# Three attention stages whose VectorE and ScalarE queues take the order of the source

## The chip, the cores and the metric

The program runs on one core of a Trainium2 chip, in one launch. The metric is the device time of one execution in microseconds. Before the change the median of three runs was 4061.31 us (4060.87 to 4061.83). All times below come from these runs or from one profiled execution of the kernel before.

## The reference, cut to what matters

Two blocks of two layers each work on 512 tokens and 256 context tokens of width 1024, batch 1, float32. The first layer of the first block is a recurrent mixer (RWKV); it is not touched. Behind it stand three attentions:

```python
# layer 2 of block 1 (MLA): 16 heads, 512 queries, 768 keys (tokens and context)
s = q @ k.T / sqrt(96);  p = softmax(s);  o = p @ v;  d_x = (o * silu(gate)) @ w_out

# layer 1 of block 2 (AB): 8 heads with a window of 128, 256 context keys and a sink column in the softmax,
# and 8 heads over all 768 keys; tokens (512) and context (256) are both queries; 2 kv heads in each half
q = rope(rms_norm(q) * g);  k = rope(rms_norm(k) * g)
p = softmax(concat([s_local, s_ctx, sink]));  o = p @ v;  o_lat = concat(oa, ob) @ w_out

# layer 2 of block 2 (C): 8 heads, each with two score matrices over the 768 keys
a = softmax(s[0]) - lam * softmax(s[1]);  o = rms_norm(a @ v) * (1 - lam_init);  o_lat = o @ w_out
```

Behind AB and behind C stands a mixture of 32 experts, of which each token takes two.

## The kernel before, in words

The kernel is written in a tile language. Each statement is an instruction for one engine; a planner then sets the order in which each engine's queue takes its instructions, by its own costs, and adds the semaphores. A block `with tc.manual_schedule(engines=...)` tells the planner to leave the named engines in the order of the source for what stands in the block. Before the change the three attentions name `PEO`, which is TensorE (PE) alone: PE runs in the order of the source, while VectorE (DVE), ScalarE (ACT), GpSimd (POOL) and SyncE (SP, which issues most DMAs) run in the planner's order. Other blocks of the kernel already name more engines (the products behind the attentions that lead to an expert layer name PE, DVE and ACT, L1707).

**What each attention does.** A unit of work is a *query tile of 128 rows of one head* ("item"). For it PE writes scores into a PSUM tile `S` (two of them), DVE takes the row maximum (L1261, in C L2760) and scales it (L1263, L2761), ACT makes the exponentials and their sum (L1268, L2763), DVE takes the reciprocal of the sum (L1272, L2766) and scales the probabilities (L1277, L2417, L2768). In the source these stand together, one behind the other. PE then transposes the probabilities of an *earlier* item (two items earlier in MLA and AB, one in C), DVE and ACT take turns to copy the transposes out of PSUM (L1296 on ACT, L1298 on DVE, L2778), and when a head is full PE multiplies with the values.

**What fills PE between.** `Fill` (L2069) holds generators that make the projections of the *next* pair of heads (MLA, `mla_project`), the next unit of four heads (AB, `AbUnit.all`; four units) or the next head (C, `CHead.all`; eight heads). `fill()` is called once or several times per item and issues a few matmuls each time. Where a projection tile is complete, its consumers are issued at that very place of the source: ACT copies, and in AB and C the norm of queries and keys with their rotation, `qk_split` (L2666, "the norm" below): a square on ACT (L2674), a sum on DVE (L2676), twelve short DVE instructions that follow each other (L2677, L164 to L168), a scaling (L2679), then products on DVE (L2689) and POOL (L2690, L2691) whose sum DVE takes (L2692), and a split into a high and a low part (L2693, L2694). AB has three norms in each of its first three units, C three in each of its first seven heads. Their transposes follow later (`turns`, L2286; `turns_c` and `turns_x`, L2633 on), with casts into `Q` and `K` by DVE and ACT in turn.

**The weights of C.** `CHead.all` calls `CIn.later` (L2571), which splits the weights of the head after next into a high and a low part, in four pieces:

```python
for i in range(4):
    if i:
        self.load(h, i)              # a DMA into one of two buffers (WB = 2)
    with self.g.tc.issue_after(after.ins):
        self.split(h, i)             # ACT: cast to the high part (L2546); POOL: the low part (L2547)
```

Pieces 2 and 3 can be loaded only when POOL has let go of the buffers of pieces 0 and 1. In the source the four casts stand one behind the other, ahead of the exponentials of the second query tile. The weights of AB are split by POOL (L2211, L2212), behind the last projection tile of a unit.

Of the kernel before, what the change touches and what calls it, by code (L numbers as in the profile page):

```python
# [1367 lines left out]
def fresh(g, i):  # L1368

    g.R[i] = g.place(i, [P, D], F32)  # L1370
    return g.R[i]
# [259 lines left out]
def take_in(g, into, tiles):  # L1631

    with g.tc.tile_pool(name="psIn", bufs=2, space=PSUM) as ps, g.tc.manual_schedule(engines=PEO):
        into.pre(tiles[0])
# [69 lines left out]
def last_products(g, nxt, OT, wo, tiles):  # L1704
    moe = isinstance(nxt, MoeIn)
    with g.tc.tile_pool(name="psPo", bufs=3, space=PSUM) as ps, \
            g.tc.manual_schedule(engines=PEO | ({mybir.EngineType.DVE, mybir.EngineType.Activation} if moe else set())):  # L1707
        if moe:
            nxt.finish(ps, OT, wo)
        else:  # L1710
            out_last(g, ps, OT, wo, tiles, lambda i, *ps: nxt.turn(i, *ps) if ps else nxt.pre(i))
# [141 lines left out]
def mla_layer(g, into, nxt):  # L1853
    nc, tc, I = g.nc, g.tc, g.I
    s = into
    kp = s.outs.enter_context(tc.tile_pool(name="mlK", bufs=1, reuse_waits="tile"))
    s.OT = kp.tile([P, 8, NX], F32, name="OTl")
    s.wl = kp.tile([P, D], F32, name="wl")
    with tc.tile_pool(name="mlP", bufs=2, reuse_waits="tile") as s.pp, tc.tile_pool(name="mlT", bufs=3, reuse_waits="tile") as s.pt, \
            tc.tile_pool(name="ringP", bufs=2, reuse_waits="tile") as s.ring, \  # L1860
            tc.tile_pool(name="psS2", bufs=2, space=PSUM, reuse_waits="tile") as s.pss, tc.tile_pool(name="psT2", bufs=2, space=PSUM, reuse_waits="tile") as s.pst, \
            tc.tile_pool(name="psU2", bufs=2, space=PSUM, reuse_waits="tile") as s.psu:
        s.P, s.att, s.got = {}, 0, 0
        fill = Fill()
        fill.add(mla_project(g, s), 1)
        with tc.manual_schedule(engines=PEO):
            for pr in range(8):
                fill.until(lambda: pr in s.P)
                s.att = pr
                if pr == 7:  # L1870
                    mla_out(g, s, fill, nxt)
                mla_attend(g, s, pr, fill)
            fill.drain()
    into.close()
    nxt.early()
    nxt.open()
    with tc.tile_pool(name="psPo", bufs=2, space=PSUM) as ps, tc.manual_schedule(engines=PEO):
        for i in range(2):
            nxt.pre(i)
        nxt.turn(0, ps)  # L1880
        out_last(g, ps, s.OT, lambda i: s.wl, g.R[2:], lambda i, *ps: None if ps else nxt.pre(i + 2))
        for i in range(1, 6):
            nxt.turn(i, ps)
    nxt.full()
    s.outs.close()
# [177 lines left out]


PEO = {mybir.EngineType.PE}
HIM = -4096


# [264 lines left out]
def ab_layer(g, into, nxt):  # L2333
    nc, tc, I = g.nc, g.tc, g.I
    MC = g.M2[0]
    s = into
    with tc.tile_pool(name="abO", bufs=1, reuse_waits="tile") as kp, tc.tile_pool(name="abQ", bufs=1, reuse_waits="tile") as qp:
        s.OT = OT = kp.tile([P, 8, NT], F32, name="OT")
        s.got = 0
        with tc.tile_pool(name="abP", bufs=2, reuse_waits="tile") as s.pp, tc.tile_pool(name="psS2", bufs=2, space=PSUM, reuse_waits="tile") as s.pss, \  # L2340
                tc.manual_schedule(engines=PEO):
            s.place(1)
            s.split(1, True)
            s.room = True
            cur = s.first.place(qp)
            for i in range(3):
                cur.turns(i)
            for u in range(4):
                fill = Fill()
                s.room = False  # L2350
                if u == 1:
                    s.tables(1)
                if u < 3:
                    ahead = AbUnit(s, u + 1).place(qp)
                    fill.add(ahead.all(fill), ABN)
                else:
                    ahead = None
                    s.back()
                    ring = [s.ring.tile([P, 8 * 384], F32, name="wao", tag=n) for n in ("raw", "high", "low")]
                    wo = [ring[k // 3][:, k % 3 * D:k % 3 * D + D] for k in range(8)]  # L2360
                    for k in range(8):
                        for c in range(2):
                            nc.sync.dma_start(wo[k][:, c * 512:c * 512 + 512], I["ab_out"][c][:, k])
                    hf = s.pool.tile([P, 8 * NT], F32, name="hf", tag="hT")
                    G_ = [hf[:, i * D:i * D + D] for i in range(2)]
                    for i in range(2):
                        row_bcast(g, s.psu, MC, 16, 3 - i, G_[i], "pu")

                    both = [qp.tile([P, 2 * NT], F32, name="wl", tag=n, bufs=b) for n, b in (("Qab", 3), ("Kab", 2))]
                    wl = [w[:, 0:D] for w in both]  # L2370
                    if isinstance(nxt, MoeIn):
                        nxt.prepare([w[:, D:] for w in both], s.psu, "pu", fill.later)
                    for v in range(2):
                        nc.gpsimd.tensor_tensor(out=wl[v], in0=wo[7], in1=G_[v], op=ALU.mult)
                    fill.add(out_heads(g, s.psu, OT, wo, g.R, [G_[0]] * 2 + [G_[1]] * 4, [hf[:, k * 512:k * 512 + 512] for k in range(4, 8)],
                                       lambda: min(s.got, 7) if s.got >= 6 else 0, 7), 73000)
                ab_attend(g, s, cur, ahead, fill)
                fill.drain()
                if u < 3:
                    cur = ahead  # L2380
        into.close()
        nxt.early()
        nxt.open()
        last_products(g, nxt, OT, lambda i: wl[int(i > 1)], g.R)
        nxt.full()
# [312 lines left out]
def c_layer(g, into, nxt):  # L2698
    nc, tc, I = g.nc, g.tc, g.I
    MC = g.M2[1]  # L2700
    s = into
    with tc.tile_pool(name="cK", bufs=1, reuse_waits="tile") as kp, tc.tile_pool(name="cP", bufs=2, reuse_waits="tile") as s.pp:
        s.OT = OT = kp.tile([P, 8, NX], F32, name="OT")
        with tc.tile_pool(name="psS2", bufs=2, space=PSUM, reuse_waits="tile") as s.pss, \
                tc.manual_schedule(engines=PEO):
            cur = s.first.place(s.pp)
            for h in range(8):
                fill = Fill()
                if h < 7:
                    ahead = CHead(s, h + 1).place(s.pp)  # L2710
                    fill.add(ahead.all(fill), 21000)
                else:
                    s.back()
                    last, Gx = (fresh(g, i) for i in range(2))
                    w = [s.tile("wco", n, F32).rearrange("p a k f -> p a (k f)") for n in ("low1", "low0", "high1", "high0")]
                    wo = [w[k // 3][:, k % 3] for k in range(7)] + [last]
                    for k in range(8):
                        for c in range(2):
                            nc.sync.dma_start(wo[k][:, c * 512:c * 512 + 512], I["c_out"][c][:, k])
                    row_bcast(g, s.psu, MC, 16, 2, Gx, "pu")  # L2720
                    nc.gpsimd.tensor_tensor(out=last, in0=last, in1=Gx, op=ALU.mult)
                    if isinstance(nxt, MoeIn):
                        nxt.prepare([s.pp.tile([P, 2 * NT], F32, name="rw", tag="Kc")], s.psu, "pu", fill.later)
                    fill.add(out_heads(g, s.psu, OT, wo, g.R[2:], [Gx] * 4, [w[3][:, 1 + k // 2, k % 2 * 512:k % 2 * 512 + 512] for k in range(4)],
                                       lambda: 0 if s.left else 7, 7), 48000)
                if h == 0:
                    cur.turns_c()
                    for _ in range(16):
                        fill.one()
                    cur.turns_x()  # L2730
                c_attend(g, s, h, cur, fill)
                fill.drain()
                if h < 7:
                    cur = ahead
            c_finish(g, s)
        into.close()
        nxt.early()
        nxt.open()
        last_products(g, nxt, OT, lambda i: last, g.R[2:])
        nxt.full()  # L2740
# [668 lines left out]
```

## Time and profile before

| what | value |
|---|---|
| time, median of 3 runs | 4061.31 us |
| profiled execution: its own time | 4052.4 us |
| profiled execution: span from first to last instruction | 4050.6 us |
| MLA attention, 1476 to 1826 us of the span | 350 us, PE busy 333.1, DVE 211.4 |
| AB attention, 1902 to 2281 us | 379 us, PE busy 345.0, DVE 270.9 |
| C attention, 3015 to 3409 us | 394 us, PE busy 352.3, DVE 256.9 |

The span is read along one clock that starts with the first instruction. An engine's busy time is the time in which at least one of its instructions ran; what is left is time in which it waited. The granted clock of TensorE (PEclk) is the mean share of its full speed in a stretch. In the timeline, the bracket behind an instruction is the idle time of its engine ahead of it and what ended it.

### The profile page before, as it was taken

How to read it: one execution, taken by the hardware profiler on the slowest of the kernel's cores; microseconds unless marked ns; L12 is line 12 of the kernel's file. 1: busy time of each engine (PE TensorE's matmuls, PEld its weight loads, DVE VectorE, ACT ScalarE, POOL GpSimd, SP SyncE). 2: the span in 40 equal slices, each digit the busy share in tenths (PEclk: the TensorE clock that was granted, in tenths of full speed). 3: DMA queues.
4: the chain of work that ended last, by engine and by line, in shares of the span. 5: the costliest groups of instructions: out<-in, count | busy, mean ns of one | idle time of the engine just before them, and what ended most of it. 6: DMA issues, size and time to landing. Idle time of an engine off the chain costs nothing. (4 is left out here: it accounts for less than half of the span.)

```text
span 4050.6 us, 83636 instructions
## 1 busy us (share of the span) xinstructions
PE 3554.0 (88%) x34840; PEld 2257.8 (56%) x34840; DVE 2120.0 (52%) x5084; ACT 1285.9 (32%) x3117; POOL 756.0 (19%) x745
## 2 busy tenths in 40 slices
PE   7699899989878889997899789999868888999998
PEld 4677777777764467656775432232268884322322
DVE  6434544455455666648885643333377774433333
ACT  3243344334322354424443211111145542111110
POOL 1100000000001111121211233333232221322221
PEclk9799998999978899998999899999979998999999
DMA  6865565666564110112011489999731123999995
GB/s 210 232 187 187 180 201 179 207 197 194 187 200 136 69 58 31 42 65 72 23 46 36 161 322 371 394 380 377 264 99 43 48 88 133 351 384 375 374 372 213
DMA packets 282440, 778.76 MB, mean 192 GB/s; under 512 B 62348, under 2 KB 183244, under 8 KB 255820
## 3 DMA queue, kind: packets, MB, share of 16 engines
q1 hardware_dynamic: 258460, 710.63, 49.0%
q0 software_dynamic: 19552, 56.67, 5.0%
q8 instruction: 275, 4.51, 0.5%
q10 hardware_dynamic: 4048, 6.10, 0.4%
q14 instruction: 105, 0.86, 0.1%
HBM read 715.57 MB, written 71.86 MB: 194 GB/s over the span
## 5 line engine op out<-in xcount | busy, mean ns | idle before, releaser
L3189 PE MATMUL H<-wex,xT 128*32 128x512 f32 x3072 | 561.3, 609 | 56.1 <-DMA wex<-in_w 50.9
L3190 PE MATMUL H<-wex,xT 128*32 128x512 f32 x1024 | 539.1, 610 | 11.4 <-DMA wex<-in_w 11.4
L3192 PE MATMUL H<-wex,xT 128*32 128x512 f32 x2048 | 537.2, 602 | 0.0
L3148 PE MATMUL Y<-wex,uT 128*32 128x512 f32 x2048 | 507.9, 596 | 2.9 <-issue 1.7
L3189 PEld LDWEIGHTS H<-wex,xT 128*32 128x32 f32 x3072 | 127.4, 112 | 329.8 <-issue 260.4
L3161 DVE TENSOR_TENSOR yo<-R,Y 64x512 f32<-64x512 f32 x128 | 87.4, 684 | 388.5 <-PE Y L3148 201.7
L3154 PE MATMUL Yc<-wex,uT 128*32 128x512 f32 x1024 | 288.0, 614 | 0.0
L3090 POOL DMA_INDIRECT xg<-hbuf,rq x192 | 184.5, 961 | 544.6 <-DVE xT L3098 420.8
L411 PE MATMUL pd<-dw,dl 128*128 128x128 f32 x1536 | 249.7, 307 | 33.9 <-DMA dl<-Ld 24.3
L3192 PEld LDWEIGHTS H<-wex,xT 128*32 128x32 f32 x2048 | 121.2, 112 | 243.1 <-issue 236.5
L411 PEld LDWEIGHTS pd<-dw,dl 128*128 128x128 f32 x1536 | 210.0, 210 | 54.7 <-DMA dl<-Ld 21.4
L411 PE MATMUL pd<-dl,dw 128*128 128x128 f32 x1344 | 215.9, 297 | 5.4 <-issue 1.7
L1268 ACT ACTIVATE prob<-S,smx 128x768 f32<-128x768 f32 (+3 forms) x160 | 125.7, 786 | 237.0 <-DVE smx L1263 208.7
L1206 DVE COPY RT<-ZU 32x128 f32<-32x128 f32 x192 | 54.4, 283 | 260.9 <-PE ZU L411 233.6
L411 PEld LDWEIGHTS pd<-dl,dw 128*128 128x128 f32 x1344 | 175.8, 198 | 27.1 <-issue 10.2
L2611 PE MATMUL pu<-wc,hT 128*128 128x384 f32 (+1 forms) x768 | 181.4, 324 | 0.0
L3117 ACT COPY uT<-puT 128x384 f32<-128x384 f32 x64 | 30.7, 479 | 469.4 <-PE puT L3115 469.4
L3166 DVE TENSOR_TENSOR yo<-R,Yc 32x512 f32<-32x512 f32 x128 | 87.6, 684 | 166.1 <-PE Yc L3154 165.1
L1261 DVE TENSOR_REDUCE smx<-S 128x1 f32<-128x768 f32 (+3 forms) x160 | 128.8, 805 | 69.1 <-PE S L1999 38.3
L3098 DVE STREAM_TRANSPOSE xT<-xg 128x768 f32<-128x768 f32 (+1 forms) x68 | 102.9, 1514 | 114.2 <-PE H L3192 92.5
L3106 ACT ACTIVATE th<-H 128x512 f32<-128x512 f32 x64 | 38.2, 597 | 374.8 <-PE H L3190 367.4
L1231 ACT ACTIVATE RT<-SY,PC 64x64 f32<-64x64 f32 x368 | 93.8, 303 | 152.8 <-PE SY L411 148.1
(623 smaller groups left out, 7950.8 us busy)
## 6 DMA issues: line engine op xcount, KB each, us to landing
wex<-in_w SPq DMA_DIRECT2D x186, 2048.0 KB, 13.9
dl<-Ld SPq DMA_DIRECT2D x180, 512.0 KB, 4.1
wmod<-in_mod_w SPq DMA_DIRECT2D x128, 512.0 KB, 4.8
dw<-in_rw_in SPq DMA_DIRECT2D x30, 512.0 KB, 7.4
wex<-in_w POOLq DMA_DIRECT2D x6, 2048.0 KB, 11.3
wcr<-in_c_in SPq DMA_DIRECT2D x28, 384.0 KB, 4.1
Ld<-lerp SPq DMA_DIRECT2D x18, 512.0 KB, 6.0
lerp<-in_mod_w SPq DMA_DIRECT2D x8, 1024.0 KB, 13.1
```

Of the source, the lines that this page charges most:

```text
L411: return g.nc.tensor.matmul(out, **kw)
L1231: ev = nc.scalar.activation(nrt[h, d, ni if d == 0 else 3 - ni, e, :], Sp[h, d, :], AF.Copy, scale=PC[h, d, cc[d]:cc[d] + 1])
L1261: nc.vector.tensor_reduce(m[:, 0:1], S[:, :n], mybir.AxisListType.X, ALU.max)
L1268: nc.scalar.activation(p[:, :n], S[:, :n], AF.Exp, scale=scale, bias=m[:, 1:2], accum_out=m[:, 2:3])
L2611: nc.tensor.matmul(o, lhsT=x, rhs=w[:, a:3, kb, :], start=kb == i == 0, stop=kb == 7 and i == 2)
L3090: own.gather = nc.gpsimd.indirect_dma_start(out=xg[:, a], out_offset=None, in_=quarters, in_offset=bass.IndirectOffsetOnAxis(ap=own.rq[:, ...
L3098: own.turned = nc.vector.transpose(xT[:, a:a + n].rearrange("p a k t -> p (a k) t"), xg[:, a:a + n].rearrange("p a (i k) -> p a k i", k=8))
L3148: mm(self.Y[h][q(self.lb + a)], lhsT=self.uT[:, fb, q(a)], rhs=self.w2[:, fb, 512 * h:512 * h + 512], start=fb == 0, stop=fb == 3)
L3154: mm(self.Yc[q(self.hb + h)], lhsT=self.uT[:, fb, q(2)], rhs=self.w2[:, fb, 512 * h:512 * h + 512], start=fb == 0, stop=fb == 3)
L3189: mm(H1[q(to)], lhsT=xT[:, a, kb, :], rhs=w[0][:, kb, :], **f)
L3190: mm(H1[q(lb + 1)], lhsT=xT[:, 2, kb, :], rhs=w[1][:, kb, :], **f)
L3192: mm(H3[q(hb + a)], lhsT=xT[:, a, kb, :], rhs=w[1][:, kb, :], **f)
```

## The change

In the three places where an attention's block is opened, the set of engines that keep the order of the source grows from PE to PE, DVE and ACT. POOL and SP stay with the planner. No instruction is added or taken away by the text of the change; what stands ahead of the blocks and behind them is planned as before.

```diff
@@ mla_layer
-        with tc.manual_schedule(engines=PEO):
+        with tc.manual_schedule(engines=PDA):
             for pr in range(8):
                 fill.until(lambda: pr in s.P)
@@
 PEO = {mybir.EngineType.PE}
+PDA = PEO | {mybir.EngineType.DVE, mybir.EngineType.Activation}
 HIM = -4096
@@ ab_layer
-                tc.manual_schedule(engines=PEO):
+                tc.manual_schedule(engines=PDA):
             s.place(1)
             s.split(1, True)
@@ c_layer
-                tc.manual_schedule(engines=PEO):
+                tc.manual_schedule(engines=PDA):
             cur = s.first.place(s.pp)
             for h in range(8):
```

## Rows read from the trace of the kernel before

**Rows 1.** Busy time by stretch: three stages, one MLA pair, one AB unit.
```profile
core 0: us, PE busy (x) PEld busy (x) DVE busy (x) ACT busy (x) POOL busy (x), PEclk, DMA share, GB/s
...
1476.00:1826.00 350.00, 333.09 (x1762) 230.01 (x1761) 211.35 (x477) 145.29 (x279) 53.35 (x44) 0.98 0.14 45
1902.00:2281.00 379.00, 345.00 (x2045) 257.94 (x2044) 270.86 (x772) 144.84 (x370) 75.84 (x83) 0.94 0.09 29
3015.00:3409.00 394.00, 352.34 (x2107) 300.46 (x2106) 256.89 (x769) 175.36 (x447) 91.70 (x100) 0.95 0.19 53
1513.00:1553.00 40.00, 37.09 (x213) 26.79 (x213) 25.21 (x54) 17.96 (x35) 6.15 (x4) 1.00 0.09 30
1902.00:1987.00 85.00, 73.38 (x484) 62.28 (x483) 69.13 (x214) 34.68 (x94) 20.87 (x30) 0.89 0.05 14
```

**Rows 2.** DVE timeline, AB (start, us, instruction, idle before): reciprocals behind 513, 768, 256 columns.
```profile
1905.89 0.16 DVE L1272 RECIPROCAL smx<-smx 128x1 f32<-128x1 f32 x1 [0.91 <-ACT prob L1268]
...
2162.89 0.16 DVE L1272 RECIPROCAL smx<-smx 128x1 f32<-128x1 f32 x1 [1.14 <-ACT prob L1268]
...
2185.36 0.16 DVE L1272 RECIPROCAL smx<-smx 128x1 f32<-128x1 f32 x1 [0.72 <-ACT prob L1268]
```

**Rows 3.** DVE waits over AB: who, for whom, total us, times, longest.
```profile
DVE smx L1272 <- ACT prob L1268: 28.4, 36, 1.4
```

**Rows 4.** DVE timeline ahead of AB: a norm nearly alone, with two casts.
```profile
1891.36 0.81 DVE L2676 TENSOR_REDUCE qss<-qsq 128x10 f32<-128x640 f32 x1
1892.20 0.43 DVE L2313 CAST Kab<-pT 64x256 fp32r<-64x256 f32 x1
...
1893.48 0.69 DVE L2306 CAST Qab<-pT 128x512 fp32r<-128x512 f32 x1
...
1900.32 0.69 DVE L2694 TENSOR_TENSOR qsp<-qsp 128x512 f32<-128x512 f32 x1
```

**Rows 5.** POOL and DVE timeline, AB: the weight split beside the norm.
```profile
1963.18 7.29 POOL L2212 TENSOR_TENSOR wablow<-wab,wabhigh 128x768 fp32r<-128x768 f32 x4
...
1919.59 0.17 DVE L166 SCALAR_TENSOR_TENSOR rst_qk<-rsy_qk 128x10 f32<-128x10 f32 x1
...
1965.06 1.73 DVE L166 SCALAR_TENSOR_TENSOR rst_qk<-rsy_qk 128x10 f32<-128x10 f32 x1
```

**Rows 6.** ACT timeline, C: the four casts of a head's weights.
```profile
3065.29 1.58 ACT L2546 CAST wc<-wcr 128x768 fp32r<-128x768 f32 x2
...
3072.16 0.83 ACT L2546 CAST wc<-wcr 128x768 fp32r<-128x768 f32 x1 [0.19 <-DMA wcr<-in_c_in]
...
3074.76 0.83 ACT L2546 CAST wc<-wcr 128x768 fp32r<-128x768 f32 x1 [1.32 <-DMA wcr<-in_c_in]
```

**Rows 7.** DVE timeline, the same head of C.
```profile
3072.01 0.17 DVE L2766 RECIPROCAL smx<-smx 128x2 f32<-128x2 f32 x1 [1.87 <-ACT prob L2763]
...
3076.91 0.69 DVE L2676 TENSOR_REDUCE qss<-qsq 128x8 f32<-128x512 f32 x1 [3.43 <-ACT qsq L2674]
...
3080.55 1.82 DVE L2760 TENSOR_REDUCE smx<-S 128x1 f32<-128x768 f32 x2
...
3084.16 0.41 DVE L2694 TENSOR_TENSOR qsp<-qsp 128x256 f32<-128x256 f32 x1
...
3090.22 0.96 DVE L2760 TENSOR_REDUCE smx<-S 128x1 f32<-128x768 f32 x1 [0.34 <-PE S L2758]
...
3104.63 0.17 DVE L2808 TENSOR_SCALAR oss<-oss 128x4 f32<-128x4 f32 x1 [0.67 <-ACT osq L2786]
```

**Rows 8.** PE waits: over AB (the first), over C (the others).
```profile
PE ppT L1292 <- DVE prob L2417: 12.7, 8, 3.1
...
PE pT L2630 <- DVE qsp L2694: 13.5, 10, 5.6
PE pT L2630 <- DVE Qc L2643: 12.7, 14, 2.1
```

**Rows 9.** PE busy, PEclk, DMA share, GB/s: the end of an AB unit.
```profile
1964.00:1990.00 26.00, 16.60 (x97) 0.67 0.17 58
```

## The prediction

> **What bounds the kernel now.** I read the busy times by stretch first, then the waits of PE and DVE inside each attention, then the timelines of DVE and ACT beside the order of the source. The stretches [rows 1] show PE busy for 333 of 350 us in MLA, 345 of 379 in AB and 352 of 394 in C, so PE is the bound of all three and all that a better order could win there is its idle time, 17, 34 and 42 us. What matters for this change is the second column to look at: DVE is busy for 69.1 of the 85 us of an AB unit and 25.2 of the 40 us of an MLA pair [rows 1]. It is the next engine behind PE, and it has 15.9 us to spare in the AB unit.
>
> DVE stays below its limit because the planner shuffles it. In the source the reciprocal of an item stands right behind its scaled maximum, with ACT's exponentials between them. Where the trace has them so, DVE stands idle for 0.91 us (513 columns), 1.14 us (768) or 0.72 us (256) [rows 2]. AB has 96 items. At some 0.95 us each that is 91 us of waiting, yet only 36 such waits with 28.4 us are in the trace [rows 3]. The other 60 have another instruction in the hole: a reduction of the next item, a copy of transposes, a piece of the norm. Keeping the source's order opens these holes again.
>
> **The change part by part.** It removes no instruction. It moves DVE's and ACT's, and each term below is what the moved order makes of one stage. POOL and SP are still planned, but they serve what DVE and ACT now do later.
>
> *AB, first three units.* Per unit, in the order of the source, DVE needs its busy time of 69.1 [rows 1], and beside it:
> - the holes: 24 items, 8 each of 513, 641 and 257 columns, at 0.91, about 1.0 (between 0.91 and 1.14) and 0.72 [rows 2], 21.0 us, in which nothing else may run;
> - the norms: one ran nearly alone ahead of the stage, from 1891.36 to 1901.01 with two foreign casts of 0.43 and 0.69 in it [rows 4], so 8.5 us in a block. Its instructions, all dependent, lose the overlap that neighbours give each other, and its sum waits for POOL's products. I take 1.7 us more per norm than its share of the busy time, 5 us per unit, and 1 us per norm for the square on ACT, which now stands behind an exponential, 3 us;
> - the same lost overlap in the items, an estimate of 0.2 us for each of 24, 5 us.
>
> That is 69.1 + 21 + 5 + 3 + 5 = 103 us against a unit of 85. PE's 73.4 us [rows 1] fit inside; DVE becomes the bound, and a unit grows by 18 us. The second unit gets 3 us more: its rotation tables are fetched by a DMA of ACT's queue at the unit's start, and DVE now has to stand there for it (an estimate; no row has this wait, between 0 and 6 us). The third unit has wider items (4 x 1.14 + 2 x 0.72 = 6.0 us of holes for six), so 24 us of holes but no weight split, and I take 17. The fourth has no norms and is filled by PE with the output products; I give it 2. AB: 18 + 21 + 17 + 2 = 58, rounded to +60. Bounds: without the estimates the holes and the busy time alone make 90 against 85, which over three units is +15; with a full 8.5 us for each norm and items of 3 us, 24 x 3 + 25.5 + 15 for copies = 112, it is +85.
>
> The weight split of POOL runs beside the last norm of the first two units, and there a DVE instruction that takes 0.17 us elsewhere took 1.73 us, while four POOL subtractions took 7.29 us [rows 5]. [...]
>
> *C, heads 0 to 5.* Here ACT's new order is as dear as DVE's. The four weight casts stand together in the source ahead of the exponentials of the second tile. Two run at 3065.29 for 1.58 us, but the third could start at 3072.16 and the fourth at 3074.76, each just when its DMA had landed [rows 6]; the planner put both exponentials between. In the source's order ACT is shut from 3066.9 until 3075.6, and as a copy of 0.7 us moves ahead of the casts, until 3076.3. I follow one head from there:
> - Two exponentials, 1.9 us with their sums: 3078.2. The reciprocal, at 3072.01 before [rows 7], comes at 3078.4; to the scaled rows about 1.5 us more (an estimate: the longest of its four instructions covers 768 columns, like a reduction of 0.96 us): 3080.
> - The norm started at 3076.91. Its first part took until 3080.55, 3.6 us; the rest, to 3084.57, 4.0 us with 1.82 us of foreign reductions inside [rows 7]. Alone it is 3.6 + 2.2 + 1.0 for POOL's products = 6.9 us. It ends at 3087, and only then may DVE reduce the third tile, at 3080.55 before: +6.5.
> - That tile needs 4.8 us (two reductions 1.9, hole 1.1, tail 1.5, the rest between them): 3091.8. The second norm's square stands on ACT behind the product of the tile before, which waits for copies that wait for these exponentials; by the same steps 3094.4. The norm ends at 3101.4, where the fourth tile's reduction follows, at 3090.22 before [rows 7]: +11.
> - 4.8 us to 3106.2, the small norm of the context 4.3 us in a block (an estimate: twelve dependent instructions at 0.17 and a gap, as in [rows 5], and five of 256 columns), then the two casts of Q that the planner had set inside it, and K, the last transposes, the last product: the sum of squares at 3104.63 [rows 7] comes at about 3117.4, +13; the root behind it now precedes the cast of K that the next head's scores need, 2.9 us more (ten such instructions and one of 512 columns, 0.7): +15.7.
>
> PE's 42 us of idle time in C cannot cover this, for the chain DVE - ACT - PE - DVE is closed within a head. Nothing in it was allowed to overlap, so I take 14 for each of six heads, 84. Head 6 has norms but no casts: 15.7 less 6.4, taken as +8. Head 7 has neither: +2. C: +94. Bounds: only the holes and the ACT block that PE does not already wait through, about 3 us per head, +20; the chain in full and one more wait of 2 us per head, 6 x 18 + 14 = +122.
>
> *MLA.* DVE's own 25.2 us in a pair of 40 [rows 1] plus 8 holes of 1.14 [rows 2], 9.1 us, and about 2 us of waits for ACT's copies make 36.3; PE has 37.1 [rows 1]. Two engines equally full, two score buffers between them: neither is clearly the bound. I take +2 us for each of seven pairs and +2 for the last: +16. Below, the planner's own misplacements go and it is -5; above, each pair loses 5 us, +40.
>
> *Sum.* 60 + 94 + 16 = +170 us. From the profiled execution, 4052.4 (span 4050.6), that is 4222; its difference from the median, 8.9 us, lies outside the change, so I add 170 to 4061.3: 4231, given as 4230. The bounds together: 15 + 20 - 5 = +30 (4091) and 85 + 122 + 40 = +247 (4308).
>
> **The rivals.**
>
> *A, faster.* The source's order is the one PE's order was written against, and where the planner served a norm first PE waited: 12.7 us for scaled probabilities in AB, 13.5 and 12.7 us for norms and Q casts in C [rows 8]. If these 38.9 us go and nothing comes, the time is 4022. It decides where DVE's reopened holes fit into its idle time. For it: these waits are real. Against it: 21 us of holes meet 15.9 us of idle time in an AB unit, and in C the source puts the Q casts later still. Chance 0.05.
>
> *B, the cover holds but for C's casts.* If PE lets DVE fall behind and the two score tiles absorb the holes, only ACT's shut 6.4 us per head remain, 6 x 6.4 = 38: 4100. For it: DVE is idle for 137 of 394 us in C [rows 1]. Against it: the norms are in series with the scores. Chance 0.08.
>
> *C, the clock falls too.* Where PE waited long, at the end of an AB unit, it was busy for 16.6 of 26 us and its granted clock was 0.67 [rows 9], against 0.94 to 0.98 over the stages. If AB's first units and C fall to about that, PE's links of C's chain, some 16 us per head (an estimate: its scores, transposes and products and the fill between them), take 16 x (0.95 / 0.67 - 1) = 6.7 us longer, 47 over seven heads: 4277. [...] Chance 0.15.
>
> *D, the order hardly changes.* The planner's order may be the source's in all that counts. The 60 missing holes speak against it. 4061, chance 0.02.
>
> **How the numbers follow.** My forecast has 0.70, of which its own range is 4150 to 4305. The range given reaches from 4115, which leaves out A, B and D (0.15), to 4310, which takes in C and the upper bounds. A measurement can tell about 0.2%, 8 us, from no change. Faster 0.05 (A), same 0.02 (D), slower 0.93.
>
> **What would show it.** Right: over AB the waits of reciprocals for exponentials rise from 28 us towards 90; an AB unit with norms lasts 100 us or more with PE busy for about 75; in C exponentials start right behind a cast that waited for a DMA, a norm runs unbroken on DVE, and a head lasts some 58 us instead of 45. Wrong: units of 85 us with these waits in place (PE covers them), a third cast that does not wait, or PE's busy time in a stage up by the clock alone.

## The result and the profile after

The changed kernel takes 4315.58 us (median of 4309.16, 4315.58 and 4333.93) against 4061.31: ratio 1.064 [1.0618, 1.0662], 254 us slower. The direction was forecast; the time is 5.6 us above the top of the range and 86 above the point.

I cut both spans at the first row maximum of every MLA pair, AB unit and C head. The stages then lose (us):

| stage | before | after | more | forecast, bounds |
|---|---|---|---|---|
| MLA, seven pairs | 270.6 | 316.1 | +45.5 | +16 with the last pair, -5 to +40 |
| AB, first three units | 256.5 | 357.9 | +101.4 | +56 |
| AB, fourth unit | 120.1 | 133.9 | +13.8 | +2 (all of AB +60, +15 to +85) |
| C, eight heads | 394.4 | 486.2 | +91.8 | +94, +20 to +122 |

That is 252.5 of the 263 us between the two profiled spans; the rest lies ahead of the stages, between them and in MLA's last pair. So C came as forecast, and MLA and AB went past their upper bounds. The busy times after, to be read against [rows 1] (three stages, an MLA pair, two AB units, a C head):

```profile
core 0: us, PE busy (x) PEld busy (x) DVE busy (x) ACT busy (x) POOL busy (x), PEclk, DMA share, GB/s
1484.10:1879.50 395.40, 348.39 (x1758) 234.28 (x1757) 213.58 (x478) 142.81 (x279) 55.71 (x45) 0.96 0.13 41
1958.60:2450.40 491.80, 377.61 (x2034) 273.43 (x2033) 292.28 (x770) 141.50 (x369) 73.56 (x83) 0.86 0.07 22
3187.40:3673.60 486.20, 381.42 (x2106) 327.59 (x2106) 270.23 (x784) 175.48 (x448) 88.26 (x100) 0.88 0.15 42
1573.90:1618.60 44.70, 38.36 (x213) 26.61 (x213) 25.39 (x54) 17.60 (x35) 4.94 (x3) 1.00 0.09 27
1958.60:2079.10 120.50, 86.16 (x517) 70.24 (x517) 77.94 (x216) 33.62 (x95) 17.04 (x22) 0.82 0.06 18
2079.10:2195.30 116.20, 79.61 (x473) 62.81 (x472) 76.74 (x210) 33.61 (x95) 18.38 (x27) 0.82 0.06 18
3301.40:3362.70 61.30, 46.39 (x272) 42.98 (x272) 35.14 (x105) 23.75 (x60) 12.87 (x14) 0.86 0.14 35
```

In no unit is an engine full. In the second AB unit DVE is busy for 76.7 of 116 us and PE for 79.6. The holes opened as foretold: the waits of reciprocals for exponentials over AB went from 28.4 [rows 3] to 89.9 us (forecast 90). But they are 22 us of a unit, and DVE is idle for 40.

```profile
DVE smx L1272 <- ACT prob L1268: 89.9, 96, 1.1
DVE smx L1261 <- PE S L2409: 32.9, 24, 4.5
DVE OT L2442 <- ACT OT L2442: 17.3, 9, 4.4
```

What the sums hide shows when that unit is cut where its norms lie (2089 to 2103, 2123 to 2135 and 2157 to 2172 hold one each):

```profile
2079.00:2089.00 10.00, 8.61 (x57) 7.85 (x56) 6.08 (x18) 3.89 (x10) 2.38 (x9) 1.00 0.00 0
2089.00:2103.00 14.00, 6.72 (x42) 5.72 (x40) 11.16 (x32) 2.41 (x9) 2.94 (x5) 0.92 0.00 1
2103.00:2113.00 10.00, 8.94 (x50) 8.65 (x51) 5.73 (x18) 3.97 (x12) 0.00 (x0) 0.78 0.00 0
2113.00:2123.00 10.00, 7.95 (x55) 4.98 (x56) 6.67 (x23) 4.38 (x15) 0.00 (x0) 1.00 0.02 5
2123.00:2135.00 12.00, 8.14 (x57) 6.82 (x55) 9.98 (x26) 1.38 (x4) 2.81 (x5) 0.99 0.04 9
2135.00:2147.00 12.00, 9.50 (x49) 6.37 (x50) 7.56 (x21) 5.01 (x14) 0.00 (x0) 0.73 0.00 0
2147.00:2157.00 10.00, 9.20 (x67) 8.08 (x67) 5.29 (x17) 3.92 (x12) 2.10 (x3) 1.00 0.06 15
2157.00:2172.00 15.00, 2.75 (x22) 1.55 (x18) 13.61 (x25) 1.20 (x4) 8.25 (x6) 0.67 0.31 105
2172.00:2182.00 10.00, 6.44 (x30) 5.22 (x30) 4.95 (x15) 3.58 (x10) 0.00 (x0) 0.64 0.00 0
2182.00:2195.00 13.00, 11.18 (x56) 7.38 (x57) 5.73 (x19) 3.86 (x12) 0.00 (x0) 0.61 0.05 12
```

The two engines largely take turns. In the three norms, 41 us together, DVE is busy for 34.8 us and PE for 17.6; in the other 75 us PE is busy for 61.8 and DVE for 42.0. The norm that stops PE longest is the third, beside which POOL splits weights: four of its ten-column instructions take 0.93 to 1.72 us instead of 0.17. That stretch as a timeline of PE and DVE:

```profile
2156.66 2.43 PE L2437 MATMUL po<-pX,Vab 128*64 128x256 f32 x20
2158.24 0.81 DVE L2677 TENSOR_REDUCE qss<-qsq 128x10 f32<-128x640 f32 x1
...
2160.04 1.72 DVE L164 TENSOR_SCALAR rsy_qk<-qss 128x10 int32<-128x10 int32 x1
...
2170.18 0.42 DVE L1298 COPY pC<-ppT 128x256 f32<-128x256 f32 x1
2170.75 0.66 PE L2437 MATMUL po<-pC,Vab 128*64 128x128 f32 x2 [11.66 <-DVE S L2416]
```

PE's next product needs the copy `pC`, and that copy stands behind the whole norm in DVE's queue: 11.66 us for an instruction of 0.42. (The releaser named is the instruction behind the copy; the copy is the one PE's product reads.) The first norm of the unit stops PE by way of ACT. An exponential waits for the row maximum that stands behind the norm in DVE's queue, ACT's copy of transposes stands behind that exponential, and PE's next transposes wait for the copy:

```profile
2103.18 0.48 ACT L1268 ACTIVATE prob<-S,smx 128x257 f32<-128x257 f32 x1 [9.77 <-DVE smx L1263]
...
2104.06 0.69 PE L1292 MATMUL ppT<-cst,prob 128*128 128x128 f32 x2 [7.74 <-ACT pX L1296]
```

Over the first three units PE waits 34.0 us for such copies by ACT, 48 us for instructions in DVE's queue, and only 3.1 us for a free score tile.

MLA has no norm, but the same shape within a pair. The same view of one pair, cut where its last softmax ends and the gate's matmuls begin:

```profile
1573.90:1606.60 32.70, 27.22 (x146) 18.14 (x145) 21.46 (x46) 15.83 (x32) 4.94 (x3) 1.00 0.07 19
1606.60:1618.60 12.00, 11.13 (x67) 8.46 (x68) 3.93 (x10) 1.77 (x3) 0.00 (x0) 1.00 0.12 48
```

In the first part DVE's 21.5 us and eight holes of 1.12 make 30.4 of 32.7; in the second DVE waits for PE, which has its last matmuls to do one behind the other. The granted clock is 1.00 in both, so it has no part in this pair's length.

### The profile page after: what moved, and what is told of

Same layout as the page of the kernel before. It is cut to its first block, busy times and chain, and to the rows that moved or that the text cites. A ratio compares the mean times of both kernels' runs of the same rounds, so it can differ in the third digit from the quotient of the medians.

```text
span 4313.7 us, 83626 instructions
## 1 busy us (share of the span) xinstructions
PE 3636.1 (84%) x34840; PEld 2352.3 (55%) x34840; DVE 2152.3 (50%) x5084; ACT 1278.0 (30%) x3117; POOL 750.8 (17%) x745
## 5 line engine op out<-in xcount | busy, mean ns | idle before, releaser
L3190 PE MATMUL H<-wex,xT 128*32 128x512 f32 x3072 | 585.2, 607 | 54.4 <-DMA wex<-in_w 49.8
L3191 PE MATMUL H<-wex,xT 128*32 128x512 f32 x1024 | 538.0, 608 | 8.7 <-DMA wex<-in_w 8.6
L3193 PE MATMUL H<-wex,xT 128*32 128x512 f32 x2048 | 539.7, 601 | 0.0
L3190 PEld LDWEIGHTS H<-wex,xT 128*32 128x32 f32 x3072 | 149.8, 112 | 307.4 <-issue 219.6
L411 PE MATMUL pd<-dw,dl 128*128 128x128 f32 x1536 | 249.0, 307 | 35.1 <-DMA dl<-Ld 24.6
L3193 PEld LDWEIGHTS H<-wex,xT 128*32 128x32 f32 x2048 | 122.2, 111 | 227.0 <-issue 210.7
L411 PEld LDWEIGHTS pd<-dw,dl 128*128 128x128 f32 x1536 | 209.5, 209 | 55.8 <-DMA dl<-Ld 21.7
L1292 PE MATMUL ppT<-cst,prob 128*128 128x128 f32 x784 | 131.8, 298 | 70.4 <-ACT pX L1296 35.7
L2612 PE MATMUL pu<-wc,hT 128*128 128x384 f32 (+1 forms) x768 | 190.3, 336 | 0.0
L1292 PEld LDWEIGHTS ppT<-cst,prob 128*128 128x128 f32 x784 | 97.1, 150 | 120.3 <-ACT pX L1296 40.6
```

The costliest lines, as they stand in the source:

```text
L411: return g.nc.tensor.matmul(out, **kw)
L1292: nc.tensor.transpose(pp[:, k, :], p[:, (i + k) * P:(i + k + 1) * P], g.C("ident"))
L2612: nc.tensor.matmul(o, lhsT=x, rhs=w[:, a:3, kb, :], start=kb == i == 0, stop=kb == 7 and i == 2)
L3190: mm(H1[q(to)], lhsT=xT[:, a, kb, :], rhs=w[0][:, kb, :], **f)
L3191: mm(H1[q(lb + 1)], lhsT=xT[:, 2, kb, :], rhs=w[1][:, kb, :], **f)
L3193: mm(H3[q(hb + a)], lhsT=xT[:, a, kb, :], rhs=w[1][:, kb, :], **f)
```

## Experiments

Theory 1 was that each reopened hole and each block comes on top of what DVE waited for before. Its rivals are in the expectations. Ratios are against the kernel before, run beside each (4058 to 4061 us). The last three columns are mean lengths, cut as above, of MLA's first seven pairs, AB's first three units and C's heads 1 to 5.

| kernel | time, us | ratio to before | pair | unit | head |
|---|---|---|---|---|---|
| before | 4061.3 | | 38.7 | 85.5 | 45.1 |
| the change | 4315.6 | 1.064 [1.0618, 1.0662] | 45.2 | 119.3 | 61.4 |
| only_mla | 4099.8 | 1.0099 [1.0069, 1.0129] | 45.2 | 85.6 | 45.5 |
| only_ab | 4177.0 | 1.0284 [1.0267, 1.0301] | 38.7 | 120.1 | 44.8 |
| only_c | 4165.7 | 1.0269 [1.0250, 1.0288] | 38.7 | 85.8 | 61.6 |
| pe_dve | 4292.2 | 1.0583 [1.0563, 1.0603] | 47.2 | 115.7 | 58.1 |
| pe_act | 4164.4 | 1.0253 [1.0231, 1.0275] | 41.4 | 91.4 | 54.6 |
| filled | 4275.8 | 1.0532 [1.0512, 1.0552] | 43.1 | 110.8 | 60.2 |
| filled_planned | 4107.0 | 1.0116 [1.0097, 1.0135] | 38.9 | 85.7 | 51.0 |
| warm | 4367.0 | 1.0748 [1.0728, 1.0768] | 45.1 | 129.7 | 64.4 |
| woven | 4258.0 | 1.0483 [1.0457, 1.0509] | 43.1 | 108.6 | 59.7 |
| woven2 | 4215.7 | 1.0380 [1.0355, 1.0405] | 43.1 | 103.6 | 55.4 |
| woven_dve | 4180.2 | 1.0302 [1.0283, 1.0322] | 39.1 | 99.6 | 57.4 |
| woven_mla | 4201.0 | 1.0349 [1.0327, 1.0370] | 42.1 | 102.3 | 55.6 |
| no_norms | 4244.0 | 1.0469 [1.0444, 1.0494] | 45.2 | 91.7 | 61.6 |
| no_norms_planned | 4050.8 | 0.9973 [0.9959, 0.9988] | 38.7 | 79.4 | 45.3 |
| no_norms_filled | 4163.5 | 1.0266 [1.0247, 1.0286] | 43.1 | 83.2 | 55.8 |

**One stage at a time** (`PDA` in one of the three blocks).

```diff
-        with tc.manual_schedule(engines=PEO):
+        with tc.manual_schedule(engines=PDA):     # only_mla; the other two stay PEO
```

> Only the MLA stage keeps the source's order on VectorE and ScalarE; AB and C are planned as before. Theory 1 (each stage's loss is its own: the reopened holes of its softmaxes and its unbroken blocks come on top of VectorE's other waits): the stage loses what it lost in the full change, +45 us over its pairs and +6 us ahead of its first scores, AB and C stay as before, 4061 + 52 = 4113 us. Rival (what a late MLA leaves behind is made up by the planned AB stage, or some of AB's loss came from MLA): 4061 to 4090.

> Only the AB stage keeps the source's order. Theory 1: its first three units last about 120, 116 and 121 us instead of 85, the fourth 134 instead of 120, and nothing else moves: 4061 + 115 = 4176 us. Rival (the loss needs the slower stages around it, through the planned POOL and SP work): some 60 us as predicted, 4121.

> Only the C stage keeps the source's order. Theory 1: heads of 61 us instead of 45 and a stage longer by 92 us: 4061 + 92 = 4153 us. Rival as for the other two: less, down to 4100 (only the casts' block).

Ratios of 1.0099, 1.0284 and 1.0269 against the 4058.7 us measured beside them are 40, 115 and 109 us, together 264 against 254 for the full change. MLA came 13 us under what was expected, AB on it, C 13 above. Each stage's loss is its own, and the lengths of pairs, units and heads in the table are those of the full change.

**One engine at a time.**

```diff
-PDA = PEO | {mybir.EngineType.DVE, mybir.EngineType.Activation}
+PD = PEO | {mybir.EngineType.DVE}            # pe_dve, in all three blocks
+PA = PEO | {mybir.EngineType.Activation}     # pe_act, in all three blocks
```

> All three stages keep the source's order on VectorE, while ScalarE is planned as before. Theory 1 (VectorE's order is what costs in MLA and AB; in C ScalarE's casts cost 6.4 us of a head): MLA +50, AB +115, C +92 - 38 = +54: 4061 + 219 = 4280 us. Rival 2 (ScalarE's order is what costs: TensorE waits 34 us for ScalarE's copies of transposes in the first three AB units and hardly for VectorE's): MLA +20, AB +50, C +20, 4150 us. Rival 3 (it takes both orders together, since the planner can work round one): below 4130.

> All three stages keep the source's order on ScalarE, while VectorE is planned as before. Theory 1 (VectorE's order carries the loss; ScalarE's counts only where C's casts wait for their DMA, as the 23 us between the full change and VectorE's order alone say): MLA 0, AB 0 to +10, C +25: about 4095 us. Rival 2 (in-order ScalarE is dear by itself and the two orders share one loss): MLA +20, AB +50, C +50, 4180 us.

DVE's order carries the loss in AB: 30 of the 34 us of a unit. But ACT's order costs 105 us by itself, three times what theory 1 gave it: 2.7 us of a pair, 6 of a unit, 9.5 of a head. In C the two orders alone are worth 13.0 and 9.5 us of a head and together 16.3, so they share a part of the loss. In MLA DVE's order alone is worse than both (47.2 us against 45.2).

**Holes filled, casts moved to POOL.** In the source, an item's reciprocal and scaling go behind the next item's reduction.

```diff
-        A.p, r = softmax(g, s.pt, S, NT, scale, None, 3)
-        scale_rows(g, A.p, NT, r)
+        A.p, m = softmax(g, s.pt, S, NT, scale, None, 3, behind)   # calls behind() after the exponential
+        behind.left = A.p, m, NT            # its reciprocal and scaling: in the next softmax; AB alike
@@ CIn.split
-        nc.scalar.copy(hi, w)
+        (nc.gpsimd.tensor_copy if h else nc.scalar.copy)(hi, w)
```

> The full change, with the source itself altered in two places: in MLA and AB the reciprocal and the scaling of an item stand behind the reduction of the next item, so that VectorE works while ScalarE has the exponentials; in C GpSimd makes the four weight casts of a head instead of ScalarE. Theory 1 (the holes come on top of VectorE's other waits and go away in full; the cast block costs 6.4 us of a head): MLA pairs 45 to 38.5, AB units 120 to 100, C heads 61.4 to 55: 4315 - 49 - 64 - 38 = 4165 us. Rival (VectorE then waits for TensorE instead, at the transposes and the next scores, so a filled hole only moves the wait): pairs 43, units 115, C 60: 4285 us.

> The same altered source, VectorE and ScalarE planned as before the change. Theory 1 (the planner had already filled the holes, and had moved the casts round the exponentials): 4061 us, within 15. Rival (the source's order steers the planner too, and the altered one is better by the 28 us of holes that were left in AB, the 12 in MLA and the casts): 4020 us.

Theory 1 fell. The 22 us of holes are gone from a unit, and the unit is 8.5 us shorter; of 9 us a pair gets 2.1. In the first three AB units DVE now waits for scores (the same view as above; the columns are total us, times and the longest):

```profile
DVE S L2435 <- PE S L2431: 20.0, 11, 4.3
DVE smx L1261 <- PE S L2428: 18.5, 16, 4.5
```

In C 1.2 us of a head were gained in the mean, but nearly all of it in the one head of five that had no casts beside it (56.4 us; the others have 60.5 to 61.9). Under the planner heads became 6 us longer. The casts had been given to an engine beside which DVE ran slower (groups of the head from 3314 us: busy us, mean ns; first the kernel with casts on POOL, then the change):

```profile
L2782 DVE TENSOR_REDUCE smx<-S 128x1 f32<-128x768 f32 x8 | 7.6, 950 | 3.6 <-PE S L2780 3.6
L2715 DVE TENSOR_SCALAR qsp<-qsp 128x256 int32<-128x256 int32 x5 | 3.7, 748 | 0.2
L2716 DVE TENSOR_TENSOR qsp<-qsp 128x256 f32<-128x256 f32 x3 | 2.8, 918 | 0.1
```

```profile
L2761 DVE TENSOR_REDUCE smx<-S 128x1 f32<-128x768 f32 x8 | 7.6, 951 | 5.2 <-PE S L2759 5.2
L2694 DVE TENSOR_SCALAR qsp<-qsp 128x256 int32<-128x256 int32 x5 | 1.8, 351 | 0.2
L2695 DVE TENSOR_TENSOR qsp<-qsp 128x256 f32<-128x256 f32 x3 | 1.3, 425 | 0.1
```

These two groups of the norm take twice as long (748 ns against 351, 918 against 425), the reduction of the scores as long as before (950 and 951 ns). So this run says nothing on the price of the casts on ACT.

**More work for PE.**

```diff
@@ AbUnit.tile (16, for units behind the first), CHead.tile (8 alike)
+                for i in range(16):
+                    nc.tensor.matmul(p[:, 0:384], lhsT=hi[:, 0, :], rhs=whi[:, 0, :], start=i == 0, stop=i == 15)
```

> The full change with needless matmuls ahead of each projection tile of the units behind the first, 16 of 384 columns in AB and 8 of 256 or 384 in C (their sums are overwritten): some 16 us more of TensorE's work in an AB unit and 7 in a C head, to see what the lower granted clock (0.82 and 0.86) costs. Rival 3 (the clock is a good part of the loss): it goes to 0.95 or more, AB units 120 to 110, C heads 61 to 57: 4315 - 30 - 24 = 4260 us. Theory 1 (VectorE's order sets the time, whatever the clock): the clock rises and the units stay within 3 us, heads within 2: 4305 to 4330 us.

Both were wrong. Over the first AB unit and two C heads:

```profile
1958.10:2092.90 134.80, 103.86 (x610) 89.53 (x609) 77.90 (x215) 33.77 (x95) 17.05 (x22) 0.84 0.05 16
...
3401.60:3463.70 62.10, 51.13 (x320) 47.55 (x320) 35.21 (x105) 23.57 (x60) 12.90 (x14) 0.95 0.13 35
3463.70:3531.20 67.50, 54.59 (x320) 51.21 (x320) 35.14 (x105) 23.88 (x60) 12.88 (x14) 0.87 0.12 32
```

The clock hardly rose in AB's first two units (0.82 to 0.84), so what it costs there was not learnt. A C head at 0.95 was no shorter than the change's at 0.86, but had 8 matmuls more in each tile; against heads of its own run the clock does show, for the same 320 matmuls took 62.0 and 62.1 us where it was 0.94 or 0.95 and 64.8 to 67.6 where it was 0.87 to 0.89. What the run also shows is that needless work (17.7 us in the first unit, 103.86 less 86.16) made the three units 14.5, 10.3 and 6.4 us longer, although PE had been idle for 34 us of the first. Most of the work that PE is given here does not fall into its waits. That, and the cuts above, led to theory 4: PE's and DVE's work meet in fixed phases, and the phases add up.

**Norms cut into pieces.** `qk_split` becomes a generator, and each softmax of the following items takes one piece behind its exponential.

```diff
     nc.scalar.activation(p[:, :n], S[:, :n], AF.Exp, scale=scale, bias=m[:, 1:2], accum_out=m[:, 2:3])
+    weave(g)                                 # next of five pieces of the norm; in woven2 in C too
@@ CIn.later
+            if fill and i > 1:
+                fill.later(lambda i=i: self.split(h, i), 9)
+                continue
-MPF = 15500
+MPF = 21000                                  # woven and woven_mla only: PE's order in MLA
```

> The full change, with the source altered: in AB each norm is cut into five pieces and one piece stands in the hole of each following item, between the scaled maximum and the reciprocal; in C the casts of the third and fourth weight piece stand nine fill steps later; in MLA the projection of the next pair is spread a third faster over the pair (TensorE's order). Theory 4 (TensorE's and VectorE's work meet in fixed phases, a norm's 8.5 us in which TensorE runs out of released work and fill stretches in which VectorE does, and the phases add up): AB units 120, 116 and 121 to 105, 102 and 110, C heads 61.4 to 57.5, MLA pairs 45 to 43: 4315 - 40 - 24 - 14 = 4237 us. Rival 5 (the place of the norms does not matter; VectorE's order waits as long in sum, as with the holes filled): units within 4 of the full change, heads 61: about 4300 us.

> As the last one, but MLA's projection as in the change, the norms of C cut into pieces too (two pieces in each tile's softmax), and in MLA and AB the reciprocal and the scaling behind the next item's reduction, as in the kernel with filled holes. Theory 4 (both kinds of phase are evened out): MLA pairs 43, AB units about 98, C heads 53: 4315 - 15 - 62 - 55 = 4183 us. Rival 5 (no more than filling the holes gave): MLA 43, AB 110, C 60: 4275 us.

> The kernel with filled holes, cut norms and later casts, with VectorE in the source's order and ScalarE planned as before the change. If ScalarE's order is a part of the loss by itself (+6 us in an AB unit and +2.8 in an MLA pair where it alone was kept): AB units of about 104 us to 98, C heads 55 to 52: 4216 - 18 - 18 = 4180 us. Rival (once VectorE's order is evened out ScalarE waits for nothing that matters, and the planner moves copies behind VectorE's back, as in MLA where VectorE's order alone was worse than both): 4216 to 4230.

> The kernel with filled holes, cut norms and later casts, and MLA's projection of the next pair spread a third faster over the pair. Theory 4 (phases that add up: filling the holes shortens VectorE's phase by 2 us, the faster projection takes 2 us out of TensorE's phase at the end of the pair, and the two gains add): pairs 45 to 41, everything else as without it: 4216 - 13 = 4203 us. Rival (both take the same 2 us): pairs 42.8, 4216 us.

The place of the norms matters: cutting took 10.7 us off a unit of the change (woven), cutting and filled holes together 15.7 (woven2), and in C cutting took another 4.3 off a head. The 10.7 hold some filling, since the pieces stand in holes (the reciprocals' waits in the first three units fall from 66.0 to 42.4 us); with holes filled on both sides cutting is worth 7.2 (110.8 to 103.6). Theory 4 had the direction and about three quarters of the size in total. In MLA filling gave 2.1, the faster projection 2.1, both 3.1 and not 4, so they overlap in part. woven_dve met its total by accident: it gained 4.0 us in a pair, where it was not foreseen, and lost 2.0 in a head, where 3 were expected back.

In woven's head from 3309 us the later casts let the second tile be ready 7.6 us sooner (from 19.5 to 11.9 us behind the head's start), but they and POOL's part of them now fell into the norm, which went from 7.6 to 10.8 us; 2.6 us were left at that head's end, and 1.7 in the mean of heads 1 to 5.

**Norms left out.**

```diff
@@ AbUnit.norm
+        if self.u:
+            self.sp[i] = s.pt.tile([P, 2, 5, 2, 64], F32, name="qsp", tag="qsp5", bufs=2)
+            s.g.nc.gpsimd.memset(self.sp[i], 0.0)
+            return
```

> The full change without the norms of AB's units behind the first (their results are left out; GpSimd writes zeros in their place), so nothing of them is on VectorE or ScalarE. Theory 4 (each norm is a phase of 8.5 us that adds to the unit, since TensorE runs out of work in it): 3 x 8.5 = 26 us less, units of 120, 116 to about 93, the third (its norms are those of the fourth unit) 121 to 95: 4315 - 78 = 4237 us. Rival 6 (the copies' order and the holes keep VectorE behind anyway): units of 108: 4280 us.

> The kernel before the change without the same norms, VectorE and ScalarE planned. Theory 4 (under the planner the norms lie in VectorE's idle time, and TensorE's 76 us set the unit): 85 to 80, 4059 - 16 = 4043 us. Rival (a norm costs the planned kernel its own length too): units down to TensorE's 76 us, 4030 us.

> The kernel with filled holes and later casts (4216 us with its cut norms, AB units of 104 us) without the same norms. Theory 4 (holes and norms are all that costs in AB): units of 85, 4216 - 56 = 4160 us. Rival 6 (the order of the copies carries the rest): units of 95 or more, 4190 us.

Theory 4 was right in all three, within 8 us. The second unit in the change's order, under the planner, and with holes filled:

```profile
2048.60:2138.20 89.60, 75.89 (x473) 62.06 (x473) 50.86 (x152) 31.76 (x92) 16.40 (x20) 0.89 0.08 23
```

```profile
1993.90:2072.00 78.10, 72.53 (x494) 60.65 (x493) 51.79 (x151) 32.40 (x92) 14.13 (x11) 0.96 0.07 21
```

```profile
2028.90:2107.00 78.10, 69.16 (x473) 57.45 (x472) 50.44 (x151) 31.94 (x92) 16.48 (x20) 0.96 0.07 20
```

A norm takes 8.6 us of DVE ((76.7 - 50.9) / 3). In the source's order three of them, with their squares and products, cost the unit 119.3 - 91.7 = 27.6 us, 9.2 each: their whole length. Under the planner they cost 85.5 - 79.4 = 6.1, 2.0 each. The 33.8 us of a unit are then 27.6 - 6.1 = 21.5 from the norms and 91.7 - 79.4 = 12.3 without them; filling the holes takes 8.5 of these (91.7 to 83.2). The last 3.8 were not split further, but leaving ACT to the planner gave back about as much (119.3 to 115.7 in pe_dve, 103.6 to 99.6 in woven_dve).

Cut norms are still dear: with filled holes a unit with them (woven2) takes 103.6 us and one without norms 83.2, so a norm in five pieces costs 6.8 us, an unbroken one 9.2 (110.8 to 83.2), and one that the planner places 2.0. Breaking the norm up is therefore not all that the planner does; what else it does was not isolated.

None of the altered sources that compute the same beats the kernel before.

## Why the prediction was right and wrong

- **PE is the bound now, DVE the next engine.** Right. That DVE has "15.9 us to spare" in a unit was read wrongly: most of that idle time was waits at fixed places, and they grew. Beside its holes DVE waited for 10 us in a unit before ((42 - 12) / 3, all its waits in the first three units less those for exponentials) and for 16 after ((113 - 66) / 3). Of these 47 us the profile puts 26 down to PE and 16 to ACT.
- **AB, the failed step.** "PE's 73.4 us fit inside; DVE becomes the bound, and a unit grows by 18 us" summed DVE over the unit, let PE's work lie beside it, and put DVE's waits for PE and for ACT's copies at nothing. The terms that it did price held: busy time, norms and lost overlap, 69.1 + 5 + 3 + 5 = 82, are 76 (mean of three units; the overlap as the trace of before has it: at 1894.09 us a ten-column instruction starts 0.08 us ahead of the end of the cast in front of it, while those of 0.17 us that follow each other in that norm start 0.19 to 0.21 us apart), the holes, put at 21, are there with 22, and the second unit's wait for its tables, put at 3, is 2.3. What is missing is those waits, 13 us in each unit by the same view ((26 + 14) / 3), and some 6 in gaps between instructions. The runs put another rule in the sum's place: PE's order is fixed, a stretch full of DVE's work stops it at the next transposes or product, and the unit comes near to a sum over such phases. By the experiments 21.5 of the 33.8 us hang on where the norms lie, and the 22 us of holes are worth only 8.5. The fourth unit's +13.8 against +2 was not studied.
- **The split beside the norm.** DVE's 1.72 us for a ten-column instruction came again, but the ten-column instructions of the norms (L164 to L168 and the scaling ahead of them, eleven in each norm) sum to 25.2 us in the first three units of before and to 27.8 now: 0.9 us more per unit, for which the forecast's sum had no term. In the norm shown above the long ones, 0.93 and three of 1.72 us, start from 2159.08 to 2163.56, while POOL's four subtractions run from 2158.00 to 2165.25; the seven from 2165.31 on take 0.17 us each. It shows plainer in C with casts on POOL, 425 to 918 ns and 351 to 748 ns. What makes an instruction of DVE longer there was not shown.
- **MLA, wrong for the same reason.** "Two engines equally full" at 36.3 and 37.1 us, "+2 us for each": the pair is 32.7 us of DVE's phase and 12.0 of PE's, +6.5. Filled holes with ACT planned took 6.1 us of it back, filled holes with PE's projection faster 3.1, with the same work in the pair: its order and not its sums set it. ACT's order was given nothing here; alone it is 2.7 us of a pair. That the two phases add up is read from one pair's rows and from these gains; no run took one phase away by itself.
- **C, right, in part by luck.** The chain of a head held step by step. Counted from a head's start, the forecast had the exponentials behind the casts at 16.4, the third tile's reduction at 27.1, the fourth's at 41.5; the heads after have 17.6, 28.5 and 42.9 (below: the third cast waited 5.49 us for its DMA, and the norm ran unbroken). Heads 1 to 5 took 16.3 us more each, where I had cut the 15.7 of the working to 14; heads 0, 6 and 7 took 7.7, 6.8 and -4.3 against 14, 8 and 2, so the stage's total came out by errors that cancel. It also holds some clock, for which the chain had no term (rival C). The link by itself was priced less well: of the 6.4 us 1.7 were seen at a head's end with two casts moved, and 3.3 with all of ACT left to the planner (61.4 to 58.1). ACT's timeline after, and then DVE's, of the head that starts at 3301.38:

```profile
3316.37 0.83 ACT L2547 CAST wc<-wcr 128x768 fp32r<-128x768 f32 x1 [5.49 <-DMA wcr<-in_c_in]
...
3318.95 0.89 ACT L2764 ACTIVATE prob<-S,smx 128x768 f32<-128x768 f32 x1
```

DVE stands with the reciprocal until these are done, and the third tile is reduced when the norm ends:

```profile
3320.85 0.17 DVE L2767 RECIPROCAL smx<-smx 128x2 f32<-128x2 f32 x1 [7.09 <-ACT prob L2764]
...
3322.31 0.68 DVE L2677 TENSOR_REDUCE qss<-qsq 128x8 f32<-128x512 f32 x1
...
3329.88 0.95 DVE L2761 TENSOR_REDUCE smx<-S 128x1 f32<-128x768 f32 x1
```

- **Rival C, the clock.** It came in part, and it cost time. PE's granted clock went from 0.89 [rows 1] to 0.82 in an AB unit, and from 1.00 to 0.86 in a C head. Beside the norm shown above, where PE was busy for 2.75 of 15 us, it is 0.67, and 0.64 and 0.61 in the two stretches behind. What the clock costs shows in only_c, where two neighbouring heads have the same instructions. A head of the kernel before, those two heads, and the first 10 us of each:

```profile
3104.60:3149.10 44.50, 40.40 (x274) 37.70 (x272) 33.93 (x104) 23.97 (x60) 13.32 (x14) 1.00 0.19 48
...
3144.30:3204.10 59.80, 44.64 (x272) 41.31 (x272) 35.26 (x106) 23.76 (x60) 12.86 (x14) 0.89 0.15 36
3204.10:3265.60 61.50, 46.35 (x272) 42.97 (x272) 35.13 (x105) 23.75 (x60) 12.86 (x14) 0.86 0.14 35
...
3144.30:3154.30 10.00, 9.83 (x58) 9.53 (x59) 5.05 (x12) 4.57 (x9) 2.70 (x2) 1.00 0.01 2
3204.10:3214.10 10.00, 9.91 (x49) 9.66 (x50) 3.63 (x9) 4.57 (x9) 1.21 (x1) 0.83 0.01 2
```

PE is full at the start of both, but gets through 58 matmuls in one and 49 in the other; DVE then waits 3.64 and 5.06 us for the second tile's scores, and the head is 1.8 us longer. AB's first unit likewise took 123.1 us at 0.77 in only_ab and 120.5 at 0.82 in the change, with the same 517 matmuls. So a part of the loss in C and in AB is the clock. In the change's head that starts at 3301.38 it was 0.54 and 0.51 in the 5 us behind two stretches of 5 us in which PE was busy for only 0.68 and 1.62 us, and 1.00 in three such stretches running, 3326.4 to 3341.4, in which PE was busy throughout. How large it is against the clock of before stays open: no head in the source's order with the same work ran above 0.89.
- **Rivals A, B and D** are out: no stage gained, and casts and holes are the smaller part.

## What to carry to other kernels

Before an engine's order is fixed, cut a unit where its long blocks lie and compare the engines there. With the order of both engines fixed, a block of 8.6 us on one of them cost the unit 9.2, whatever idle time both had over the unit. An idle share is cover only if nothing orders it; filling a wait pays only if the engine that comes next in the loop was not waited for as well (22 us of holes gave back 8.5). A planner that places the instructions of a block among the work that others wait for is worth what it saves here, 7 us for each norm of 8.6; cutting the block into five pieces by hand gave back a third of that.

## What the runs showed of the hardware

In one head with four casts of 768 columns on POOL (983 ns each) beside its four subtractions (1853 ns each), two groups of DVE's norm instructions lasted twice as long as in a head with the subtractions alone (748 ns against 351, 918 against 425), while DVE's reductions of the scores kept their 950 ns; DVE's busy time in the head was 40.8 us against 35.1. In the planned kernel a head with the same four casts moved to POOL is 6 us longer in the mean (51.0 against 45.1); that the slower DVE is the whole cause is not shown.

Two heads of the same instructions differed by 1.8 us. TensorE, busy for 9.83 and 9.91 us of the first 10 us of each, had a granted clock of 1.00 in the shorter one and got through 58 matmuls, and 0.83 in the other and 49 matmuls.
